# A four-branch inference step on one core: readiness kept by an account, two moves from SBUF to SBUF, squares from token tiles, and one gate projection moved ahead of the attention

## The chip, the cores and the metric

One Trainium2 chip, one of its cores, one launch. The metric is the device time of the execution in microseconds. The engines are called as in the profile: PE (TensorE, matmuls), PEld (its weight loads), DVE (VectorE), ACT (ScalarE), POOL (GpSimd) and SP (SyncE, which here issues most DMAs). TensorE's clock has two levels, 1.2 and 2.4 GHz; the granted clock of a stretch is given as a share of 2.4 GHz.

## The reference

One layer over 1056 tokens: 1024 of a prompt and 32 of a second sequence that has a cache of 1024 keys. Model width 1024, eight heads of 64, 32 state-space groups of 16 channels with a complex state of 64 each.

```python
hn = _rmsnorm(x, ln_g)
q, k, v, ga, u, gs = jnp.split(hn @ w_in, ...)        # six blocks of 512 columns
att = stick-breaking attention(q, k, v)               # causal, log-sigmoid sums instead of softmax
ssm_y, h_re, h_im = _ssm_branch(u, ...)               # diagonal complex scan, gelu, GLU with w_glu
att_o = _rmsnorm(att, g_att) * silu(ga)
ssm_o = _rmsnorm(ssm_y, g_ssm) * silu(gs)
out = jnp.concatenate([att_o, ssm_o], -1) @ w_out
return x + out, k, v, h_re, h_im                      # then a final rmsnorm
```

Outputs are y, k, v and the last states of both sequences.

## The kernel before

All matmuls run on fp32 data split into a high and a low part, so each product is three matmuls (high by high, low by high, high by low). The 3072 columns of `w_in` are cut into 24 blocks of 128; `ORDER` (L58) gives the order of the blocks: u0 to u3, gs0 to gs3 (the state-space branch's gate), g0 (the attention gate of head pair 0), q0, k0, v0, and then the rest during the attention. One block is one projection: `proj` (L432) runs 72 matmuls over three chunks of 256, 384 and 416 tokens, loads the weights two blocks ahead, splits the next block, and hands each chunk to an evacuation.

**Head.** `x_split` (L211) makes `xh` and `xl` from the eight transposed tiles `xr` on ACT and DVE. `x_sq` (L216) squares each `xr` tile on ACT and adds the eight squares, three additions on POOL and four on DVE. `x_rs` (L228) sums them over the partitions by nine matmuls against ones (L234), makes the reciprocal root on POOL (`rsqrt`) and spreads it to `rsx` by transposing matmuls (L243). The order of this early work is a list, `PREP` (L35). The first two blocks u0 and u1 run interleaved in `proj_first` and are evacuated without `rsx`, to be scaled later.

**State-space branch.** Channels come in four blocks m. For each, `s_tables` (L717) builds tables W, rot, dec and V on DVE; `s_mats` (L791) transposes W to WT, forms a small matrix Ms and sends it through DRAM into the Toeplitz operand Tm; `u_store` (L838) writes the evacuated u to DRAM (`ud`) and `u_load` (L889) reads it back as U with 8 time steps times 16 channels on the partitions; `s_states` (L898) multiplies WT by U on PE and scans on DVE; `s_out` (L942) multiplies Tm by U and V by the states, applies gelu and moves Y through DRAM (`yd`) to `yj`, from which ACT writes `y_nat`. After m = 3 `open_glu` (L1016) loads and splits `w_glu`, `glu` (L1060) runs three chunks, and `ssm_gate` (L1092) multiplies with the gate.

**Order.** Nothing is scheduled by a compiler: each engine runs its instructions in the order in which the program emits them. These pieces are generators ("links"). `tick` (L399) is called after each step of a projection (three matmuls); it resumes every link whose wait is over. A link waits for a flag of another link or for a number of ticks, and the numbers stand in a table written by hand, `WAIT` (L42). `slot` (L994) runs a projection with ticks; `until("G")` ticks until the GLU's weights are there.

**Attention.** `weave` (L1520) runs two streams. The main one is `pipeline`: for each head pair and each block of 256 queries scores on PE, two sigmoids on ACT, a scan on DVE, a product on POOL or DVE, transposes, a split on ACT and DVE, and the product with v. The fill is the list of the remaining projections, v1, q1, k1, g1, v2, q2, k2, g2, v3, q3, k3, g3 and the state-space half of the output projection. For each unit of main PE work the weave takes so much fill as `RATIO` (L47) says. A fill entry can wait for a flag: v2 waits for `att0`, the end of pair 0's last block, which comes two units into pair 1. `_layout` stores the blocks of `w_in` in the order of `ORDER`.

Of the kernel before, what the change touches and what calls it, by code (L numbers as in the profile page):

```python
# [15 lines left out]
D = 1024  # L16
# [25 lines left out]
WAIT = {'md': (0, 0, 6, 0), 'Tm': (11, 14, 6, 0), 'ud': (1, 1, 0, 4), 'ul': (8, 3, 1, 1), 'yd': (1, 0, 3, 2), 'yj': (5, 0, 1, 3), 'W': (1, 7, 1, 4), 'U': (8, 8, 3, 12), 'b': (2, 1, 1, 1), 'S': (1, 5, 1, 1), 'V': (4, 1, 4, 1), 'glu': (14, 11, 10), 'T': (1, 4, 3, 1), 'y': (17, 10, 16, 20), 'gate': (9, 9, 7, 8)}  # L42
# [15 lines left out]
ORDER = [f"{n}{m}" for n in "us" for m in range(4)] + [f"g{p}" for p in EARLY] + ["q0", "k0", "v0"]  # L58
for _p in range(1, 5):
    ORDER += ["v1"] if _p == 1 else []  # L60
    ORDER += [] if _p - 1 in EARLY else [f"g{_p - 1}"]
    ORDER += [f"v{_p}"] if 1 < _p < 4 else []
    ORDER += [f"q{_p}", f"k{_p}"] if _p < 4 else []


@with_exitstack
def hymba_step(ctx, tc, xT, xn, w_in, ln_g, kcT, vc, w_glu, b_glu, w_out, g_att, g_ssm, final_g,
               prm, h0, bmat, cvec, cbd, dsk, consts_in,
               y_out, kT_out, vT_out, st_out):
    nc = tc.nc  # L70
# [301 lines left out]
    for md in mds:  # L372
        nc.sync.dma_start(md[128:256], zz)
# [1540 lines left out]
```

## Time and profile before

| | us |
|---|---|
| median of three runs | 704.28 (703.28 to 706.74) |
| profiled execution, its time | 704.95 |
| its span, first to last instruction | 703.1 |
| PE busy in it | 634.0 |
| DVE busy | 508.2 |
| ACT busy | 352.7 |
| POOL busy | 241.6 |

The span is what the profile's rows add up to; 1.85 us of the profiled execution lie outside it. A busy PE is not the same as a fast one: at the lower clock the same matmul takes up to twice as long, so the granted clock is read beside the busy time.

### The profile page before, as it was taken

What the parts mean: (1) busy time and instruction counts of PE and PEld (TensorE: products, weight loads), DVE (VectorE), ACT (ScalarE), POOL (GpSimd) and SP (SyncE); (2) the same over time, 40 slices, a digit from 0 to 9 for tenths busy, and PEclk for the clock granted to TensorE, in tenths of its full rate; (3) what the DMA queues carried; (4) which work ended last, traced back from release to release, by engine and by line L of the source; (5) the groups of instructions that cost most, each with busy time, mean ns of one, the idle gap of its engine ahead of it and who ended that gap; (6) DMA issues with size and microseconds to landing.
All of it is one profiled execution on the core that took longest, in us unless ns stands there. A gap on an engine that the chain in (4) does not pass through costs nothing.

```text
span 703.1 us, 10847 instructions
## 1 busy us (share of the span) xinstructions
PE 634.0 (90%) x3834; PEld 570.9 (81%) x3834; DVE 508.2 (72%) x751; ACT 352.7 (50%) x805; POOL 241.6 (34%) x369
## 2 busy tenths in 40 slices
PE   7877699989999998999899998978987898989995
PEld 7877489878999997899798988967886676777884
DVE  5987999895154483687787768777778959785554
ACT  6533232431354563567665665546765746632332
POOL 0510110100123367253344326341317424233784
PEclk8998899998999998999999999999999899999998
DMA  8303514723621072101121012303253673527662
GB/s 299 85 31 77 154 31 119 243 87 97 194 68 43 25 259 109 48 31 57 62 80 55 30 62 80 106 13 99 64 155 100 191 250 110 172 93 220 216 191 97
DMA packets 62645, 79.14 MB, mean 113 GB/s; under 512 B 8864, under 2 KB 47072, under 8 KB 62592
## 3 DMA queue, kind: packets, MB, share of 16 engines
q1 hardware_dynamic: 56112, 66.90, 29.8%
q10 hardware_dynamic: 6480, 11.56, 5.2%
q8 instruction: 30, 0.49, 0.3%
q14 instruction: 23, 0.19, 0.1%
HBM read 51.97 MB, written 26.48 MB: 112 GB/s over the span
## 4 chain that ended last, share of the span: by engine, by line
PE 28%; DVE 11%; ACT 5%; issue 4%; POOL 1%; DMA 1%; DVEq 0%; ACTq 0%; POOLq 0%
PE pj L1625 8%; PE pj L439 7%; DVE cb L1207 4%; PE z L1625 4%; DVE wtl L97 3%; PE pv L1269 3%; PE tr L1306 2%; PE z L1162 2%; ACT wth L94 2%; DVE kv_out L97 1%; DVE betaL L97 1%; PE z L1358 1%; ACT cb L94 1%; DMA kc_raw<-in_vc 1%; DVE attT L97 1%
## 5 line engine op out<-in xcount | busy, mean ns | idle before, releaser
L439 PE MATMUL pj<-xh,w_hi 128*128 128x256 f32 (+2 forms) x456 | 159.7, 350 | 0.9 <-DVE kv_out L97 0.9
L439 PE MATMUL pj<-xl,w_hi 128*128 128x256 f32 (+2 forms) x456 | 148.8, 326 | 0.0
L439 PE MATMUL pj<-xh,w_lo 128*128 128x256 f32 (+2 forms) x456 | 148.3, 325 | 0.0
L1207 DVE TENSOR_TENSOR_SCAN cb<-cb 128x896 f32<-128x896 f32 (+8 forms) x66 | 96.6, 1471 | 4.7 <-ACT cb L94 4.6
L439 PEld LDWEIGHTS pj<-xh,w_hi 128*128 128x128 f32 x456 | 88.5, 194 | 5.6 <-issue 2.4
L439 PEld LDWEIGHTS pj<-xl,w_hi 128*128 128x128 f32 x456 | 88.2, 194 | 1.5
L439 PEld LDWEIGHTS pj<-xh,w_lo 128*128 128x128 f32 x456 | 87.6, 192 | 0.3
L97 DVE TENSOR_TENSOR wtl<-tr,wth 128x512 fp32r<-128x512 f32 (+2 forms) x86 | 53.5, 625 | 31.5 <-ACT wth L94 30.7
L94 ACT ACTIVATE cb<-z 128x512 f32<-128x512 f32 (+4 forms) x102 | 49.7, 487 | 47.9 <-PE z L1164 15.0
L1625 PE MATMUL pj<-xh,S 128*128 128x512 f32 (+3 forms) x212 | 69.5, 407 | 0.5 <-ACT w_raw L94 0.5
L97 POOL TENSOR_TENSOR betaL<-betaL,cb 128x896 f32<-128x896 f32 (+2 forms) x24 | 42.2, 1760 | 73.7 <-DVE cb L1207 54.4
L97 POOL TENSOR_TENSOR w_lo<-w_raw,w_hi 128x512 fp32r<-128x512 f32 x30 | 49.2, 1640 | 41.7 <-ACT w_hi L94 41.7
L97 POOL TENSOR_TENSOR betaS<-betaS,cb 128x128 f32<-128x128 f32 (+3 forms) x32 | 28.0, 880 | 74.0 <-DVE cb L1207 42.6
L94 ACT ACTIVATE wth<-tr 128x512 fp32r<-128x512 f32 (+2 forms) x86 | 47.2, 550 | 11.5 <-PE tr L1306 9.7
L1306 PE MATMUL tr<-ident,betaL 128*128 128x128 f32 x208 | 35.0, 288 | 13.1 <-DVE wtl L97 9.3
L1269 PE MATMUL pv<-wth,vS 128*128 128x256 f32 x160 | 43.9, 297 | 2.4 <-POOL wth L1246 2.4
L1625 PE MATMUL pj<-xl,S 128*128 128x512 f32 (+3 forms) x112 | 43.8, 394 | 0.2 <-DVE xl L97 0.2
L1625 PEld LDWEIGHTS pj<-xh,S 128*128 128x128 f32 (+2 forms) x212 | 37.7, 191 | 7.3 <-ACT w_raw L94 0.8
L1269 PE MATMUL pv<-wtl,vS 128*128 128x256 f32 x160 | 42.3, 286 | 0.0
L1306 PEld LDWEIGHTS tr<-ident,betaL 128*128 128x128 f32 x208 | 25.9, 147 | 17.8 <-DVE wtl L97 10.9
L97 DVE TENSOR_TENSOR kv_out<-pj,rsx 128x256 f32<-128x256 f32 (+2 forms) x55 | 28.2, 513 | 15.0 <-PE pj L439 13.9
L94 ACT ACTIVATE betaL<-z 128x512 f32<-128x512 f32 (+4 forms) x70 | 35.9, 512 | 0.0
(339 smaller groups left out, 1514.3 us busy)
## 6 DMA issues: line engine op xcount, KB each, us to landing
w_raw<-in_w_in ACTq DMA_DIRECT2D x44, 256.0 KB, 2.6
x<-in_xn SPq DMA_DIRECT2D x8, 512.0 KB, 5.1
yp_d<-x SPq DMA_DIRECT2D x8, 512.0 KB, 5.2
x<-yp_d SPq DMA_DIRECT2D x8, 512.0 KB, 4.4
y_out<-x SPq DMA_DIRECT2D x8, 512.0 KB, 2.9
xr<-in_xT SPq DMA_DIRECT2D x7, 528.0 KB, 8.5
wraw<-in_w_out SPq DMA_DIRECT2D x5, 512.0 KB, 6.6
ud<-uj SPq DMA_DIRECT2D x4, 532.0 KB, 5.6
```

The costliest lines, as they stand in the source:

```text
L94: nc.scalar.activation(out, in_, f, **kw)
L97: (eng or nc.vector).tensor_tensor(out, a, b, op)
L439: nc.tensor.matmul(ps[:, :n], a[:, k], b[:, k, t0:t0 + n], start=(k == 0 and f == 0), stop=(k == KT - 1 and f == 2))
L1162: nc.tensor.matmul(ps[:, :nn], a, b, start=(i == 0), stop=(i == len(mms) - 1 and mask is None))
L1207: nc.vector.tensor_tensor_scan(cc[:, ::-1], cc[:, ::-1], cc[:, ::-1], 1.0, OP.mult, OP.bypass)
L1269: nc.tensor.matmul(st["ps"][:, 0:256], vs[:, kb, 128 * h:128 * h + 128], w[:, c0:c0 + 256], start=(st["n"] == 0), stop=(st["n"] == 2 * nbl ...
L1306: nc.tensor.transpose(pp[:, c0:c0 + 128], b[:, 128 * kb:128 * kb + 128], ident)
L1358: nc.tensor.matmul(ps, a, b, start=(i % 2 == 0 and n == 0), stop=(i % 2 == 1 and n == 2))
L1625: nc.tensor.matmul(ps[:a.shape[1], :m], a, b_, start=(k == 0 and f == 0), stop=(k == 3 and f == len(mms) - 1))
```

## The change

1. Every link's wait is now a moment and not a number of ticks. A class `Clock` wraps the engines and keeps an account: for each emitted instruction it works out when its engine, operands and buffers would be free, by a price for each kind of instruction. `at(tiles)` waits until the account's PE time reaches the moment when the tiles are written; `dve()` until DVE's queue is within 1 us of empty. `tick` resumes a link as long as its wait is over. `WAIT` is gone. Where no projection runs, each tick adds 400 ns to the account's PE time.
2. u goes from `uj` to U, and Y to `yj`, by eight DMAs of one eighth each, from SBUF to SBUF, without DRAM.
3. The squares come from token tiles: nine tiles of x with tokens on the partitions are loaded into the freed `xr` buffers, and ACT squares each with a sum along the row, straight into the nine columns that `rsqrt` reads. The additions and the matmuls against ones are gone. `x_rs` is spawned at step 28 instead of 52, `angles` at 22 instead of 45.
4. `s_tables` is cut in two; the second half (rot, dec, V) has its own waits, and its tables have two buffers where needed. Small loads (kidx, bm, h0t, dst) are issued earlier. The GLU's weights are loaded and split by a link of their own before y3 is there.
5. The gate projection g1 leaves the attention's fill and runs after v0, ahead of the attention (`LATE`).

```diff
-RSS = 52
-RSW = 60
+RSS = 28
...
-PST = 45
+PST = 22
...
-WAIT = {'md': (0, 0, 6, 0), 'Tm': (11, 14, 6, 0), ...
+LATE = (1,)
+ORDER = [f"{n}{m}" for n in "us" for m in range(4)] + [f"g{p}" for p in EARLY] + ["q0", "k0", "v0"] + [f"g{p}" for p in LATE]
...
+class Clock:
...
+    def cost(self, e, f, n, out, ins, args):
+        if e == "PE":
+            if f == "transpose":
+                return 109.0
+            if ins[1].dtype == F32:
+                return max(1.77 * n, 100.0)
+            return 0.4414 * n + 6
+        if e == "ACT":
+            return 180 + 0.83 * n
...
+        if f == "tensor_tensor_scan":
+            return 80 + 2.09 * n
+        if f in ("tensor_scalar", "tensor_copy"):
+            return 90 + 0.55 * n
+        return (150 if f == "scalar_tensor_tensor" else 80) + 1.04 * n
...
+        if f == "dma_start":
+            b = 4 * size(out) * out.ap[0][1]
+            end = max(start + 2000 + b / 180, self.dma + b / 395)
+            self.dma = max(self.dma, start) + b / 395
+            self.t[e] = start + 340
...
+    def ready(self, *aps):
+        return max(self.last(self.w, *self.span(a)) for a in aps)
...
-    def x_sq(k):
-        act(xr[k], xr[k], AF.Square)
-        if 0 < k < 4:
-            tt(xr[0], xr[0], xr[k], OP.add, nc.gpsimd)
-        elif k > 4:
-            tt(xr[4], xr[4], xr[k], OP.add)
-        if k == 7:
-            tt(xr[0], xr[0], xr[4], OP.add)
+    def x_load(b):
+        m, c = blk(b)
+        xq[b] = xp.tile([128, D], F32, name="xq", tag=f"xr{b % KT}")
+        nc.sync.dma_start(xq[b][:m], xn[c])
+    def x_sq(b):
+        m, _ = blk(b)
+        nc.scalar.activation(xq[b][:m], xq[b][:m], AF.Square, accum_out=rst[:m, 1, b:b + 1])
...
         for b in range(9):
-            m, c = blk(b)
-            nc.tensor.matmul(ps[:m, b:b + 1], sq[:, c], ones, start=True, stop=True)
-        nc.vector.tensor_copy(rst[:, 1, 0:8], ps[:, 0:8])
+            if b == 1:
+                x_load(8)
+            yield at(xq[b], lead=XL)
+            x_sq(b)
         rsqrt(rsc, rst[:, 1], 1.0 / D, rst[:, 0], rst[:, 1])
-        yield RSW - now[0]
+        yield at(rsc)
...
         for t in list(tasks):
+            while True:
+                w = t[0]
+                if (w not in done) if isinstance(w, str) else (w() > nc.now()) if callable(w) else (w > now[0]):
+                    break
...
+    def at(*aps, lead=0.0):
+        return lambda: nc.ready(*aps) - lead
+    def dve(*aps):
+        return lambda: max([nc.t["DVE"]] + [nc.ready(a) for a in aps]) - BACK
...
         def u_store(m, uj):
-            UD[m] = dram.tile([8, 128, NCH], F32, name="ud", bufs=4)
-            nc.sync.dma_start(UD[m].rearrange("j p n -> p j n"), uj)
+            yield from after("X", m - 2)
+            yield at(uj, lead=300.0)
+            U = ss.tile([128, 8, NCH], F32, name="U", bufs=2)
+            for j in range(8):
+                nc.sync.dma_start(U[16 * j:16 * j + 16], uj[:, j])
...
         def s_states(m):
-            yield f"U{m}"
-            yield WAIT["U"][m]
+            yield f"u{m}"
             yield f"T{m}"
-            yield WAIT["T"][m]
             yield from after("Y", m - 2)
+            U, WT = z["U"], z["WT"]
+            yield at(U, WT)
...
-            yd = dram.tile([128, 8, NCH], F32, name="yd", bufs=2)
-            nc.sync.dma_start(yd, Y)
+            yield at(Y, lead=300.0)
             yj = ss.tile([128, 8, NCH], F32, name="yj", tag="uj", bufs=2)
-            nc.sync.dma_start(yj, yd.rearrange("(i c) g n -> (c g) i n", c=16))
+            for i in range(8):
+                nc.sync.dma_start(yj[:, i], Y[16 * i:16 * i + 16])
...
+        def glu_weights():
+            for f in ("V3", "T3", "B3"):
+                yield f
+            s2a.close()
+            gw = s1.enter_context(tc.tile_pool(name="gw", bufs=1, side="right"))
...
         def until(f):
             while f not in done:
+                nc.t["PE"] += 400.0
                 tick()
...
+        for i, p in enumerate(LATE):
+            slot(n + 3 + i, proj(GA[p], ga_evac(p, kvst)))
...
     def gate(p, **kw):
-        return [] if p in EARLY else [proj(GA[p], ga_evac(p, kvst), **kw)]
+        return [] if p in EARLY + LATE else [proj(GA[p], ga_evac(p, kvst), **kw)]
```

## Rows read from the trace of the kernel before

**Rows 1.** The profile page: the granted clock and the moved GB/s in 40 equal slices of 17.6 us, and the chain of waits by engine.
```profile
PEclk8998899998999998999999999999999899999998
...
GB/s 299 85 31 77 154 31 119 243 87 97 194 68 43 25 259 109 48 31 57 62 80 55 30 62 80 106 13 99 64 155 100 191 250 110 172 93 220 216 191 97
...
PE 28%; DVE 11%; ACT 5%; issue 4%; POOL 1%; DMA 1%; DVEq 0%; ACTq 0%; POOLq 0%
```

**Rows 2.** Busy time by stage. Columns: stretch, its length, then for each engine the busy us and the number of instructions, the mean granted clock, DMA share and GB/s.
```profile
20.00:40.00 20.00, 16.62 (x93) 15.83 (x91) 18.90 (x39) 10.21 (x15) 7.67 (x8) 0.91 0.20 53
...
40.00:100.00 60.00, 46.88 (x300) 41.66 (x300) 53.82 (x106) 19.14 (x62) 9.11 (x19) 0.86 0.32 86
100.00:160.00 60.00, 56.88 (x383) 49.83 (x384) 54.93 (x66) 21.11 (x56) 3.44 (x10) 0.96 0.42 132
160.00:265.60 105.60, 105.24 (x661) 102.65 (x661) 53.38 (x77) 48.55 (x88) 32.26 (x25) 0.99 0.35 116
265.60:640.00 374.40, 337.27 (x2070) 302.53 (x2068) 280.50 (x381) 220.93 (x518) 148.87 (x185) 0.96 0.30 94
```

**Rows 3.** The timeline of PE from 20 to 160 us, the instructions before which PE stood idle, and the matmuls against ones. Columns: start, us, line and operation, in brackets the idle us before it and what ended them.
```profile
27.59 0.57 PE L464 MATMUL z<-xl,w_hi 128*128 128x256 f32 x2 [2.74 <-DVE xl L214]
...
41.74 0.39 PE L439 MATMUL z<-xh,w_lo 128*128 128x256 f32 x1 [2.38 <-DVE w_lo L97]
...
44.92 2.35 PE L234 MATMUL tr<-ones,xr 128*128 128x1 f32 x18
...
51.56 0.71 PE L243 MATMUL tr<-ident,rsc 128*128 128x128 f32 x4 [1.28 <-POOL rsc L97]
...
61.07 1.09 PE L802 MATMUL tr<-ident,W 128*128 128x128 f32 x4 [3.58 <-DVE W L97]
...
81.71 1.15 PE L912 MATMUL tr<-U,WT 128*64 128x133 f32 x8 [6.52 <-DMA U<-ud]
...
101.44 0.63 PE L802 MATMUL tr<-ident,W 128*128 128x128 f32 x4 [0.92 <-DVE W L97]
...
154.82 1.89 PE L964 MATMUL z<-bst,V 64*128 64x133 f32 x8 [2.15 <-DVE bst L97]
```

**Rows 4.** The timeline of DVE from 8 to 62 us.
```profile
16.28 0.42 DVE L97 TENSOR_TENSOR w_lo<-w,w_hi 128x256 fp32r<-128x256 f32 x1
...
18.34 2.71 DVE L97 TENSOR_TENSOR w_lo<-w,w_hi 128x256 fp32r<-128x256 f32 x1
20.97 2.87 DVE L271 SCALAR_TENSOR_TENSOR P<-P 128x16 f32<-128x16 f32 x3
23.88 2.44 DVE L103 TENSOR_SCALAR P<-P 128x16 f32<-128x16 f32 x1
26.23 1.31 DVE L214 SCALAR_TENSOR_TENSOR xl<-xr,lng,xh 128x1056 fp32r<-128x1056 f32 x1
...
35.73 5.34 DVE L97 TENSOR_TENSOR xr<-xr,xr 128x1056 f32<-128x1056 f32 x4
```

**Rows 5.** The timeline of POOL from 0 to 110 us.
```profile
17.80 5.59 POOL L97 TENSOR_TENSOR xr<-xr,xr 128x1056 f32<-128x1056 f32 x2 [16.91 <-ACT xr L94]
...
47.61 0.65 POOL L103 TENSOR_SCALAR rst<-rst 128x9 f32<-128x9 f32 x1 [19.01 <-DVE rst L236]
...
51.31 0.20 POOL L97 TENSOR_TENSOR rsc<-rsc,rst 128x9 f32<-128x9 f32 x1
```

**Rows 6.** The timeline of ACT from 8 to 62 us: the first square of an x tile, and the last piece of `rsx`.
```profile
12.88 1.07 ACT L94 ACTIVATE xr<-xr 128x1056 f32<-128x1056 f32 x1
...
56.24 0.51 ACT L94 ACTIVATE rsx<-tr 128x416 f32<-128x416 f32 x1
```

**Rows 7.** The timeline of the SP queue from 0 to 110 us: when it issued the last x tiles, and u of the first two blocks to and from DRAM.
```profile
8.85 2.10 SPq L365 DMA_DIRECT2D xr<-in_xT  x3
...
63.46 1.26 SPq L842 DMA_DIRECT2D ud<-uj  x2
...
74.04 0.38 SPq L894 DMA_DIRECT2D U<-ud  x1
```

**Rows 8.** DMA issues of the whole run. Columns: what, queue, count, KB each, median us from issue to landing.
```profile
xr<-in_xT SPq DMA_DIRECT2D x7, 528.0 KB, 8.5
...
ud<-uj SPq DMA_DIRECT2D x4, 532.0 KB, 5.6
U<-ud SPq DMA_DIRECT2D x4, 532.0 KB, 5.6
...
md<-Ms SPq DMA_DIRECT2D x4, 64.0 KB, 1.5
```

**Rows 9.** The instructions on the tile `uj`: one group. Columns: count, shortest, median and longest in ns.
```profile
L97 DVE TENSOR_TENSOR uj<-pv,rsx x3: 197/834/877, 77.2 to 90.7; 128x384 f32<-128x384 f32 x2, 128x32 f32<-128x32 f32 x1
```

**Rows 10.** Busy time (columns as in rows 2) of one dense projection, gs3, and of the stretch from the end of k1 to the start of v2, in which g1 is the fill.
```profile
181.00:192.70 11.70, 11.70 (x75) 11.65 (x74) 2.87 (x5) 3.51 (x4) 2.82 (x4) 1.00 0.66 199
332.90:358.90 26.00, 22.78 (x147) 21.19 (x146) 19.78 (x27) 15.49 (x36) 11.13 (x11) 0.93 0.19 62
```

**Rows 11.** The timeline of PE: the first wait of the attention, and the first of pair 1.
```profile
271.92 0.80 PE L1162 MATMUL z<-kA,qA 128*128 128x512 f32 x1 [2.98 <-ACT betaL L94]
...
338.14 0.44 PE L1162 MATMUL z<-kA,qA 128*128 128x384 f32 x1 [2.41 <-ACT kA L94]
```

**Rows 12.** The timeline of POOL from 228 to 298 us: the last of the four gate products of the state-space branch.
```profile
265.44 2.47 POOL L97 TENSOR_TENSOR y_nat<-y_nat,sgs 128x1056 f32<-128x1056 f32 x1
```

More of the change, by code (lines that the diff above doesn't have):

```diff
@@ new lines, with __init__, manual_schedule, tile_pool @@
+class TimedPools:
+    def __init__(self, clock, tc):
+        self.clock, self.tc, self.nc = clock, tc, tc.nc
+    def manual_schedule(self):
+        return self.tc.manual_schedule()
+    def tile_pool(self, name, bufs=1, **kw):
+        return TimedPool(self.clock, self.tc.tile_pool(name=name, bufs=bufs, **kw), name, bufs)
+class TimedPool:
+    def __init__(self, clock, pool, name, bufs):
+        self.clock, self.pool, self.name, self.bufs = clock, pool, name, bufs
+    def __enter__(self):
+        self.ctx, self.pool = self.pool, self.pool.__enter__()
+        return self
+    def __exit__(self, *a):
+        return self.ctx.__exit__(*a)
+    def tile(self, shape, dtype, name, tag=None, bufs=None, **kw):
+        t = self.pool.tile(shape, dtype, name=name, **({} if tag is None else {"tag": tag}),
+                           **({} if bufs is None else {"bufs": bufs}), **kw)
+        self.clock.buffer((self.name, tag or name), bufs or self.bufs, t.tensor.name if hasattr(t, "tensor") else t.name)
+        return t
@@ L66, in hymba_step, with __init__, __getattr__, call @@
+class Timed:
+    def __init__(self, clock, eng, name):
+        self._c, self._e, self._n = clock, eng, name
+    def __getattr__(self, f):
+        g = getattr(self._e, f)
+        if f == "lower_ap" or not callable(g):
+            return g
+        def call(*args, **kw):
+            self._c.run(self._n, f, args, kw)
+            return g(*args, **kw)
+        return call
 @with_exitstack
@@ L291, in exp_ @@
         yield
[L292 removed]
+        ki = sa.tile([128, 16], I32, name="ki")
         nc.vector.tensor_copy(ki, t1)
@@ L715, in angles, with two, three @@
             done.add("pc")
+        sh = [128, 8, 8, 16]
+        def two(t, i, c=None):
+            a = t[:, i:i + 2].rearrange("p r q k -> p (r q) k")
+            return (a if c is None else a[:, :, c][:, :, ::-1])[..., None].to_broadcast(sh)
+        def three(t):
+            return t.rearrange("p r q c -> p (r q) c")[:, :, None, :].to_broadcast([128, 12, 8, 16])
         def s_tables(m):
@@ L756, in s_tables, with s_tables2 @@
-            z.update(cb=cb, W=W)
-            done.add(f"W{m}")
-            FT = ss.tile([128, 3, 4, 8], F32, name="FT")
+                pass
+            z.update(cb=cb, W=W, Pm=Pm, cv=cv)
+            yield at(cb, cv)
+            ts(cb[:, 1], cb[:, 1], -1.0, None, OP.mult, None, gp)
+            ts(cv[:, 1], cv[:, 1], -1.0, None, OP.mult, None, gp)
+            gp.tensor_copy(cv[:, 2], cv[:, 0])
+            done.add(f"W{m}")
+        def s_tables2(m):
+            z = M[m]
+            g = slice(4 * m, 4 * m + 4)
+            yield f"W{m}"
+            yield from after("S", m - 2)
+            Pm, cv = z["Pm"], z["cv"]
+            FT = sa.tile([128, 3, 4, 8], F32, name="FT")
```

306 lines of the change are left out of this document (173 added, 133 removed).

## The prediction, made before the changed kernel ran

> **What bounds the kernel now.** I read the stages first, because one share for the whole run hides them. From 160 to 265.6 us PE is busy 105.24 of 105.6 us at a granted clock of 0.99 [rows 2]: there PE alone sets the time, with DVE at half load, so whatever reaches PE sooner in that stretch is worth nothing by itself. Before 160 us it is another picture: PE is idle in 20 to 160 us by 3.4, 13.1 and 3.1 us, its clock is 0.91, 0.86 and 0.96, and DVE is busy 127.65 of 140 us. So I went to the timeline of PE for that stretch and took each wait with its releaser [rows 3]. Seven of them make 2.74 + 2.38 + 1.28 + 3.58 + 6.52 + 0.92 + 2.15 = 19.57 us, and every one ends with DVE, with POOL's root or with the landing of U. The chain of waits, the last view, has PE with 28% of the span [rows 1] and is followed back only as far as the attention; for the head it says nothing.
>
> The low clock belongs to the waits. In 20 to 100 us it is lowest where the waits are; where PE runs without one (160 to 265.6) it is 0.99. What it costs I estimate as busy time by missing share [rows 2]: 0.09 x 16.62 + 0.14 x 46.88 + 0.04 x 56.88 = 1.5 + 6.6 + 2.3 = 10.4 us.
>
> **Squares from token tiles.** POOL adds squares from 17.80 us on [rows 5], and in that time DVE's instructions stretch: a split of 256 columns that takes 0.42 us takes 2.71, four tiny ones 5.3 [rows 4]. From 18.34 to 26.23 DVE does what unhindered would be some 1.3 us of work, so POOL costs it 6.6 us; its own four additions cost 5.34 more. The first loss is behind PE's wait of 2.74 us (DVE's split of x starts at 26.23), the second behind the wait of 2.38 (the split of w stands behind the additions). Both go. So do the 2.35 us of matmuls against ones [rows 3].
>
> Added are nine squares on ACT with a sum along the row. The form is in no row I read; its bounds are the plain square, 1.07 us [rows 6], and twice that. I take the plain one, about what is removed; even doubled, 9 us more fit into the time that ACT is idle (busy 10.21 of 20 us and 19.14 of the next 60 [rows 2]). Added too are nine loads on SP, 4.33 MB, which wait for the split of the x tile in whose buffer they go; behind the waiting one stand only tables' loads and the u moves, needed later. The last x tile is issued by 10.95 us and lands 8.5 later [rows 7, 8], so the tokens flow from about 19.4 us; at the 299 GB/s of the page's first slice [rows 1] they need 14.5 us, until 34. A square, POOL's root (47.61 to 51.51, 3.9 us [rows 5]) and the spreading (51.56 to 56.75, 5.2 us [rows 3, 6]) then give `rsx` at about 44 us and not 56.75. If the loads ran at half that rate it would be 58, about as before; u2 and u3, two projections of 11.7 us [rows 10], cover PE until then.
>
> **u and Y from SBUF to SBUF.** Before, u of the first block is issued at 63.46 and PE has U at 81.71 [rows 7, 3]: 18.2 us for a store, a wait in ticks and a load. Now there are eight issues of 66 KB. Issues in a row took 0.63 to 0.70 us each, a single one 0.38 [rows 7]; the nearest size, 64 KB, landed in 1.5 us [rows 8]. Bounds: 8 x 0.38 + 1.5 = 4.5 and 8 x 0.70 + 1.5 = 7.1; I take 6.5, by 0.63. The account has 8 x 0.34 + 2.4 = 5.1, so PE may wait 1.4 us at each U. Four times that is 5.6 us. The Y move saves as much time, but at a place where PE does not wait [rows 2]; I cost it at nothing, hidden by the gate and q, k, v projections.
>
> The Trainium skill, "DMA: Bandwidth & Descriptors", sections "Anatomy of one DMA" and "Bandwidth", speaks against cutting a move in eight: it gives about 2.0 us fixed for each DMA and asks for large ones. Against it stand the x tiles here, of which three were issued within 2.10 us while each takes 8.5 to land [rows 7, 8]: transfers of one queue overlap. If those 2.0 us of the Trainium skill were paid eight times in a row, a move would take 16 us and the sum below would be 38 us higher.
>
> **Links by account.** PE's waits for W (3.58, 0.92), for U (6.52) and for the scan (2.15) are instructions put in PE's queue before their data were there. With `at`, PE gets projections meanwhile, of which there are enough: ten of 11.7 us. Those waits go, unless the account is ahead of the chip. It prices a scaling of u of 384 columns at 80 + 1.04 x 384 = 479 ns; the row has 834 [rows 9]. On some 12 such instructions it falls 4.3 us behind DVE. A wait puts PE behind by just as much, so waits cannot add up to more than that shortage. New waits then: 5.6 + 4.3, about 10 us (bounds 2 and 20: the faster issue and no shortage; twice both).
>
> **g1 ahead of the attention.** In front it is a dense projection, 11.7 us [rows 10], on PE where PE is the bound. Out of the attention it leaves the stretch from k1 to v2, 26.0 us with PE busy 22.78 and DVE 19.78; v2 can't move up, as it waits for `att0`. If DVE keeps all its 19.78 us, the stretch gives back 6.2; if g1's part of it goes, which I estimate as twice gs3's 2.87 (scaling, and the products of the gate), it shrinks to 14.0 and gives 12.0. I take 8.5, since the wait for kA (2.41 us [rows 11]), which is not g1's, stays and is no longer filled. The start of the attention gains: its first wait, 2.98 us [rows 11], falls while POOL still multiplies the state-space gate (at 265.44 [rows 12]), and the clock is 0.8 in that slice [rows 1], another 2 us or so. With an earlier branch and g1 in between, this is over: 4 us, bounds 0 and 5.
>
> **The sum**, against the profiled execution's own 704.95: minus 19.6 (waits), minus 2.35 (matmuls), minus 10.4 (clock), plus 10 (new waits), plus 11.7 - 8.5 (g1), minus 4 (start) = 681.9. That execution is 0.67 above the median of the runs, so I predict **681.3 us**, 3.3% faster. The new waits alone span 673 to 691; with g1's and the start's bounds the case's own range is 671 to 693.
>
> **Rivals.**
> - *DVE sets the pace anyway.* DVE is busy 91% of 20 to 160 us and all links end on it. The change takes 6.6 + 5.34, about 12 us, off it; if that is all PE gets and the other 20 us of the gain come back as idle PE between links, the time is 704.28 - 12 + 11.7 - 8.5 - 4 = 691.5, with the g1 bounds 688 to 699. For it: DVE's load. Against: PE has projections to run in the meantime, and DVE is half idle from 160 us on, so that the branch may end later without PE running dry.
> - *No change.* The same, with g1 at its dearest (+5.5) and no better start: 12 - 5.5, 697.8, and a few us more of new waits: 699 to 707.
> - *Slower: the account runs ahead of the chip.* To pass 707.8 us the new waits must grow from 10 to 36.5 us. At 0.36 us a piece that takes about 100 mispriced instructions out of the 172 that DVE runs in 40 to 160 us [rows 2]. For it: the one price that I could hold against a row is off by 74%. Against: most are of other shapes. About 712.
> - *Slower: the eight parts of a move run one after the other.* 8 x 1.5 = 12 us [rows 8] instead of 5.1, so 7 us at each of four U's, 28 instead of 5.6: 703.7; from 1.65 us a part on it is past 707.8. By the Trainium skill's 2.0 us for each DMA (the page named above) it would be 719.
>
> **How the numbers follow.** The forecast 0.60, DVE's pace 0.20, no change 0.08, account 0.08, series (1.65 us a part or more) 0.04. A measurement of this kernel tells about 0.5% (3.5 us) from no change. Faster 0.80, same 0.08, slower 0.12. The range that leaves out no more than 2 in 10 goes from 668 to 701: it takes in the first two cases, with a little below for a better g1.
>
> **What would show it.** Right: no idle of PE over 2 us between 25 and 160 us; clock there 0.95 or more; `rsx` written by 46 us; the first `s_states` matmul by 56 us; the first score matmul of the attention by 255 us although g1 stands in front of it; k1 to v2 in 16 to 20 us. Wrong: PE waits for U of more than 3 us (series), idle PE spread over 40 to 160 us with DVE above 95% (DVE's pace), or k1 to v2 above 20 us (g1's hole is dearer than I think).

## The result, and the profile after

The changed kernel takes 711.97 us (median of four runs, 708.22 to 713.85), the kernel before 703.78 on the same chip (700.90 to 706.74): a ratio of 1.0113, with 1.0076 to 1.0149 as its 95% interval. It is slower by 1.1%; 681.3 us was forecast, with 668 to 701 as the range. The profiled execution took 708.22 us (span 706.4), the lowest of the four, so its trace holds 3.3 us of the loss against the span of before (703.1), and what the other runs lose beyond that no row shows. Almost all instructions are recorded at line L212, the account's wrapper, so tiles tell the groups apart.

Busy time of the changed kernel in the stages of [rows 2], columns as there:
```profile
20.00:40.00 20.00, 13.88 (x87) 13.50 (x85) 14.32 (x63) 13.22 (x26) 0.00 (x0) 0.95 0.72 262
40.00:100.00 60.00, 55.26 (x373) 50.74 (x374) 49.12 (x75) 21.18 (x67) 8.84 (x23) 0.93 0.29 83
100.00:160.00 60.00, 56.64 (x389) 50.04 (x388) 50.06 (x60) 20.00 (x55) 3.15 (x10) 0.97 0.42 105
160.00:265.60 105.60, 99.56 (x603) 96.12 (x604) 51.60 (x76) 50.48 (x91) 32.29 (x25) 0.97 0.33 99
```
DVE is relieved in the first three (127.65 us busy before, 113.50 now) and POOL's squares are gone. Yet PE is idle by 6.1, 4.7, 3.4 and 6.0 us, together 20.3 us, about the sum of [rows 2] (3.4, 13.1, 3.1, 0.4: 20.0 us). The idle time has moved, not gone. PE's waits in 20 to 280 us (columns: instruction, releaser, us in total, times, longest):
```profile
PE z L212 <- ACT w_hi L212: 7.8, 1, 7.8
PE tr L212 <- DMA U<-uj: 3.3, 2, 2.1
PE tr L212 <- DVE W L212: 3.0, 1, 3.0
PE z L212 <- ACT Y L212: 3.0, 1, 3.0
PE z L212 <- ACT betaL L212: 2.4, 1, 2.4
PE z L212 <- ACT yh L212: 1.8, 1, 1.8
PE z L212 <- DVE yl L212: 1.3, 2, 0.9
```
They make 22.6 us, and in the same stretch the kernel before waits 23.0. Of the seven waits of [rows 3] four are gone. Three stand in another size: u2 waits 7.83 us for its split of w (2.38, and it gets going at 41.7 us in both kernels), the first W is waited for 3.03 us (3.58), and U in two places, 2.06 and 1.28 (6.52). The other entries lie behind that stretch. The largest is read on ACT's timeline:
```profile
26.29 1.06 ACT L212 ACTIVATE xq<-xq 128x1024 f32<-128x1024 f32 x1 [5.80 <-DVE P L212]
27.26 0.18 ACT L212 ACTIVATION_READ_ACCUMULATOR xq<-xq 128x1 f32 x1
...
40.00 1.04 ACT L212 ACTIVATE xq<-xq 32x1024 f32<-32x1024 f32 x1
...
41.04 1.13 ACT L212 ACTIVATE w_hi<-w_raw 128x512 fp32r<-128x512 f32 x2
```
u0 and u1 end at 33.9 us (before 39.1), and then u2 waits until 41.70 for its split of w. It stands in ACT's queue behind nine squares (1.06 us and 0.18 for the sum each), the first of them at 26.29, and behind some 4 us of tables and evacuations between them.

Where the time went, stage by stage: v0 ends at 257.2 us (before 263.4), 6.2 earlier, all of it busy time (216.94 us of PE from 20 us on, before 223.43: the matmuls against ones and some clock). Then g1 takes 12.1 us, its price in front, as forecast. The attention starts at 271.6, 2.4 us behind g1 (2.8 us behind v0 before), v1 to k1 takes 67.2 us (66.4), and the stretch from k1 to v2, which [rows 10] has at 26.0 us, takes 23.9 (counted like these 23.9, from the end of k1's last matmul, it was 26.3):
```profile
257.10:269.20 12.10, 12.10 (x79) 12.04 (x78) 5.32 (x8) 3.59 (x8) 5.95 (x4) 1.00 0.47 175
...
338.80:362.70 23.90, 15.30 (x77) 12.13 (x76) 18.83 (x23) 13.90 (x33) 7.42 (x9) 0.79 0.10 32
```
PE has 7.48 us less to do there than in the 26.0 of [rows 10], and the stretch is 2.4 us shorter. DVE keeps 18.83 of its 19.78 us, PE's wait for kA grows from 2.41 [rows 11] to 4.02:
```profile
344.42 0.44 PE L212 MATMUL z<-kA,qA 128*128 128x384 f32 x1 [4.02 <-ACT kA L212]
```

### The profile page after: what moved, and what is told of

Its sections match the earlier page's. It is cut to its first block, busy times and chain, and to the rows that moved or that the text cites. A ratio compares the mean times of both kernels' runs of the same rounds, so it can differ in the third digit from the quotient of the medians.

```text
span 706.4 us, 10910 instructions
## 1 busy us (share of the span) xinstructions
PE 631.3 (89%) x3816; PEld 565.1 (80%) x3816; DVE 499.3 (71%) x745; ACT 357.3 (51%) x817; POOL 228.7 (32%) x366
## 4 chain that ended last, share of the span: by engine, by line
PE 47%; DVE 19%; ACT 10%; POOL 7%; issue 7%; DMA 7%; SPq 2%; ACTq 0%; DVEq 0%; POOLq 0%
PE pj L212 22%; PE z L212 12%; PE pv L212 7%; PE tr L212 6%; DVE cb L212 6%; DVE wtl L212 3%; SPq L212 2%; ACT wth L212 2%; DMA xr<-in_xT 2%; DVE kv_out L212 2%; POOL rst L212 2%; DVE attT L212 2%; POOL betaL L212 1%; DMA U<-uj 1%; DMA xq<-in_xn 1%
## 5 line engine op out<-in xcount | busy, mean ns | idle before, releaser
L212 PE MATMUL pj<-xh,w_hi 128*128 128x256 f32 (+2 forms) x472 | 161.6, 345 | 1.0 <-DVE kv_out L212 1.0
L212 PE MATMUL pj<-xl,w_hi 128*128 128x256 f32 (+2 forms) x472 | 152.0, 325 | 0.0
L212 PE MATMUL pj<-xh,w_lo 128*128 128x256 f32 (+2 forms) x472 | 151.8, 324 | 0.0
L212 DVE TENSOR_TENSOR_SCAN cb<-cb 128x896 f32<-128x896 f32 (+8 forms) x66 | 100.4, 1528 | 3.6 <-ACT cb L212 3.4
L212 PEld LDWEIGHTS pj<-xh,w_hi 128*128 128x128 f32 x472 | 91.0, 193 | 4.6 <-issue 1.6
L212 PEld LDWEIGHTS pj<-xl,w_hi 128*128 128x128 f32 x472 | 90.7, 192 | 1.5
L212 PEld LDWEIGHTS pj<-xh,w_lo 128*128 128x128 f32 x472 | 89.8, 190 | 0.3
L212 DVE TENSOR_TENSOR wtl<-tr,wth 128x512 fp32r<-128x512 f32 (+2 forms) x86 | 53.6, 626 | 31.7 <-ACT wth L212 30.9
L212 ACT ACTIVATE cb<-z 128x512 f32<-128x512 f32 (+4 forms) x102 | 49.7, 487 | 51.8 <-PE z L212 23.3
L212 PE MATMUL pj<-xh,S 128*128 128x512 f32 (+3 forms) x212 | 69.1, 405 | 0.5 <-ACT w_raw L212 0.5
L212 POOL TENSOR_TENSOR betaL<-betaL,cb 128x896 f32<-128x896 f32 (+2 forms) x24 | 42.2, 1759 | 83.7 <-DVE cb L212 37.6
L212 POOL TENSOR_TENSOR w_lo<-w_raw,w_hi 128x512 fp32r<-128x512 f32 x30 | 45.5, 1516 | 62.8 <-ACT w_hi L212 62.8
L212 PE MATMUL tr<-ident,betaL 128*128 128x128 f32 x226 | 38.4, 286 | 15.8 <-DVE wtl L212 10.6
L212 ACT ACTIVATE wth<-tr 128x512 fp32r<-128x512 f32 (+2 forms) x86 | 47.3, 551 | 9.2 <-PE tr L212 6.3
L212 POOL TENSOR_TENSOR betaS<-betaS,cb 128x128 f32<-128x128 f32 (+3 forms) x32 | 27.9, 879 | 70.6 <-DVE cb L212 51.1
L212 PE MATMUL pv<-wth,vS 128*128 128x256 f32 x160 | 45.2, 303 | 2.6 <-POOL wth L212 2.6
L212 PEld LDWEIGHTS tr<-ident,betaL 128*128 128x128 f32 x226 | 27.5, 145 | 22.6 <-DVE wtl L212 13.3
L212 PE MATMUL pj<-xl,S 128*128 128x512 f32 (+3 forms) x112 | 43.7, 393 | 0.8 <-DVE xl L212 0.8
L212 PEld LDWEIGHTS pj<-xh,S 128*128 128x128 f32 (+2 forms) x212 | 37.9, 191 | 7.5 <-ACT w_raw L212 0.8
L212 PE MATMUL pv<-wtl,vS 128*128 128x256 f32 x160 | 42.9, 290 | 0.4 <-DVE wtl L212 0.4
L212 ACT ACTIVATE betaL<-z 128x512 f32<-128x512 f32 (+4 forms) x70 | 35.9, 513 | 0.0
L212 PEld LDWEIGHTS pv<-wth,vS 128*128 128x128 f32 x160 | 31.8, 199 | 3.7 <-POOL wth L212 2.9
```

Source lines behind the costliest of these rows:

```text
L212: return g(*args, **kw)
```

## The experiments

Every ratio is to the kernel before, run beside it on the same chip, with its 95% interval.

### g1: back in the attention, and alone in front

```diff
-LATE = (1,)
+LATE = ()                    # e1: changed kernel, g1 back between k1 and v2
```


> The changed kernel with g1 put back into the attention, between k1 and v2; links by account, moves in SBUF and squares from token tiles stay. Theory (g1 ahead of the attention is a loss by itself: it cost 12.1 us in front, and k1's end to v2's start only fell from 26.0 to 23.9 us): the time falls by 8 to 11 us against the changed kernel, to about 702 us, a ratio of 0.995 to 1.000 to the kernel before; k1's end to v2's start goes back to about 26 us. Rival (the prediction's: the attention pays for the gate what the front saves): the time stays within 3.5 us of the changed kernel's 712, and k1 to v2 grows by 8 us or more.

```diff
+LATE = (1,)                  # e2: kernel before, g1 behind v0
-ORDER = ... + ["q0", "k0", "v0"]
+ORDER = ... + ["q0", "k0", "v0"] + [f"g{p}" for p in LATE]
...
```


> The kernel before with that one part of the change alone: g1 runs behind v0, ahead of the attention; S5 links, DRAM round trips and squares are as before. Theory (loss by itself): 7 to 11 us slower than before, about 712 us, ratio 1.010 to 1.015, g1 about 12 us in front and k1 to v2 still over 22 us. Rival (neutral): ratio within 0.5% of 1, k1 to v2 about 16 to 18 us.

e1: 1.0015 (0.9987 to 1.0043) of before, so 1.0% below the changed kernel. e2: 1.0082 (1.0051 to 1.0112). Both say the same: g1 in front is a loss of 6 to 7 us, between the two expectations and clear of "neutral". In e2 the stretch from k1 to v2 takes 22.8 us (26.3) with DVE busy 17.75, so what it gives back is 3.5 us and not 8.5. The start of the attention did gain there: v1 begins 0.3 us behind g1 (2.8 behind v0), v1 to k1 takes 62.8 us, and from v0's end to k1's end it is 77.1 us, only 8 more than before (69.2) although g1 lies in it. In the changed kernel it is 81.6, and the gain is missing: the last gate product ends at 271.8 us, before at 267.9. That is not because the whole branch is late, for the third product ends at 262.0 us, 2.3 earlier than before. POOL of the changed kernel:
```profile
259.55 2.46 POOL L212 TENSOR_TENSOR y_nat<-y_nat,sgs 128x1056 f32<-128x1056 f32 x1 [1.26 <-PE tr L212]
...
268.14 1.30 POOL L212 TENSOR_TENSOR w_lo<-w_raw,w_hi 128x512 fp32r<-128x512 f32 x1 [4.88 <-ACT w_hi L212]
269.40 2.42 POOL L212 TENSOR_TENSOR y_nat<-y_nat,sgs 128x1056 f32<-128x1056 f32 x1
```
The fourth product stands behind a split of the next weights, on POOL, and its sigmoid behind the other half of that split on ACT (267.43), for whose load ACT sat 2.03 us.

### The moves of u and Y

```diff
+            ud = dram.tile([8, 128, NCH], F32, name="ud", bufs=4)
+            nc.sync.dma_start(ud.rearrange("j p n -> p j n"), uj)
+            yield at(ud[0:8], lead=500.0)
-            for j in range(8):
-                nc.sync.dma_start(U[16 * j:16 * j + 16], uj[:, j])
+            nc.sync.dma_start(U, ud.rearrange("j (c g) n -> (j c) g n", g=8))
...                                              # e4: the same for Y; e6: u alone
```


> The changed kernel with u and y moved through DRAM again, as in the kernel before (one DMA out, one back, each link resumed by the account when the first should be there). Theory (the eight issues for each move hold SP for 6 us and the buffer of uj is held by them): VectorE's wait of 6.13 us at 59.5 us goes, the last W of chunk m = 0 is done before 62 us instead of 64.8, and the time is 0 to 5 us lower than the changed kernel's. Rival (the prediction's: SBUF to SBUF is the shorter way): each move lands 3 to 5 us later than in the changed kernel, and the time is 2 to 8 us higher.

> The changed kernel with u alone through DRAM; y goes from SBUF to SBUF, and g1 stays in front. Theory (it is the move of u, whose eight issues for each chunk hold SP and the two buffers of uj while the projections still write u): most of the gain of the run with both through DRAM comes, a ratio of 1.000 to 1.004 to the kernel before. Rival (it is the move of y, which makes the branch's tail long): 1.008 to 1.012, like the changed kernel.

e4: 1.0001 (0.9978 to 1.0023), 1.1% below the changed kernel and more than the theory's 0 to 5 us, so the two moves through SBUF together are a loss. The issues and landings of the changed kernel, then of e4 (columns as in [rows 8]):
```profile
U<-uj SPq DMA_DIRECT2D x32, 66.5 KB, 2.7
yj<-Y SPq DMA_DIRECT2D x32, 66.5 KB, 2.5
```
```profile
ud<-uj SPq DMA_DIRECT2D x4, 532.0 KB, 5.1
U<-ud SPq DMA_DIRECT2D x4, 532.0 KB, 3.5
```
And the changed kernel's SP queue and DVE in 48 to 66 us:
```profile
51.84 12.43 SPq L212 DMA_DIRECT2D U<-uj  x16
```
```profile
49.13 3.60 DVE L212 TENSOR_TENSOR uj<-uj,rsx 128x384 f32<-128x384 f32 x6 [0.97 <-ACT rsx L212]
...
59.46 0.64 DVE L212 TENSOR_TENSOR uj<-z,rsx 128x256 f32<-128x256 f32 x1 [6.13 <-DMA U<-uj]
...
63.57 1.23 DVE L212 TENSOR_TENSOR W<-W,tW 128x1024 f32<-128x1024 f32 x1
```
The sixteen parts of the first two blocks take 12.43 us of the queue, with a stop of 2.2 us behind the eleventh. `uj` has two buffers, and u2's scaling, third in turn, waits until the last part of u0 has landed: DVE sits 6.13 us, and the three instructions of the first W stand behind it (done at 64.8 us, before the change 60.9). In e4 a store frees `uj` in one piece, that wait is not there, W is done at 58.8, the first states come at 67.2 us instead of 73.7, and the last `y_nat` ends at 191.8 instead of 196.8. A Y move is no shorter in SBUF: from the last gelu to `y_nat` 8.1 us (186.4 to 194.5), in e4 7.5.

The Trainium skill, "DMA: Bandwidth & Descriptors", sections "Anatomy of one DMA" and "Bandwidth", asked for large DMAs because of a fixed time of each. Its figure of about 2.0 us is given for DMAs that GpSimd issues; here SP issues them. These traces don't show it paid eight times in a row: the move of u0 took 7.6 us, not 16, since parts overlap. What they show is the queue and the buffer held meanwhile.

e6 has neither expectation: 1.0202 (1.0179 to 1.0225), slower than with both moves in SBUF. Up to 118 us it runs as e4; then the first Y is thought to land sooner than it does. ACT and DVE of e6:
```profile
126.99 2.07 ACT L212 ACTIVATE y_nat<-yj 128x1024 f32<-128x1024 f32 x1 [2.66 <-DMA yj<-Y]
```
```profile
137.05 0.29 DVE L212 TENSOR_TENSOR Ms<-Ms,dd 32x128 f32<-32x128 f32 x1 [5.67 <-ACT Ms L212]
```
`y_nat` stands on ACT ahead of evictions of the next states, Ms comes later, and DVE, with the small instruction on Ms at its head, sits 5.67 us (e4: 1.00) with S of the second block behind it. S of the last block ends at 186.5 us, in e4 at 171.4. The early gain of e4 is in e6 too (first states at 67.5 us) and did not make it faster. So the wait at `uj` alone does not explain e4, and no run shows that u's move by itself is a loss.

### Squares later, and squares as before

```diff
-XL = -1500.0
+XL = -7000.0          # e3: changed kernel; e7: with g1 back and both moves through DRAM
```


> The changed kernel with the account's start of the squares of x put 5.5 us later, so that ScalarE's queue has the split of w for the third u projection ahead of most of them. Theory (ScalarE's order makes TensorE's wait of 7.83 us at 41.7 us): that wait falls below 4 us, u2 ends 3 to 6 us earlier, and the time falls by 3 to 6 us if the stage that follows is not held by something else. Rival (the S5 chain on VectorE and its DMAs set the end of the stage): the wait falls but the first score matmul comes no more than 1.5 us earlier, since later waits grow by the same.

> The run with g1 back and both moves through DRAM, and the squares of x 5.5 us later in the account as in the third experiment. Theory (the squares' place on ScalarE only shifts a wait: TensorE's wait for the split of w at 41 us shrinks by 5 us or more, but rsx and with it the first W come later by as much): within 3 us of the run with g1 back and both moves through DRAM. Rival (the third experiment lost its 12 us to the moves of u alone, and the later squares are a gain once those are gone): 3 to 6 us faster than that run.

> Links by account alone: g1 back, both moves through DRAM, and the squares of x taken from the transposed tiles on ScalarE with adds on GpSimd and VectorE and the nine sums over TensorE, as in the kernel before. What is left of the change is the account, with the small loads moved ahead. Theory (the squares from token tiles give the 5 us by which the first two u projections end earlier, of which half is lost again at ScalarE): 2 to 4 us slower than the run with g1 back and both moves through DRAM, a ratio of 0.993 to 0.997 to the kernel before. Rival (the squares' part is worth nothing or is a loss, by the wait of 7.83 us at ScalarE): as fast as that run or up to 4 us faster.

e3: 1.0244 (1.0214 to 1.0275). PE's largest hole is cut to a third, u2 ends 5 us earlier, and the kernel is 1.3% slower than the changed one. PE of e3, and its busy time in 180 to 200 us:
```profile
37.33 0.39 PE L212 MATMUL z<-xh,w_hi 128*128 128x256 f32 x1 [2.64 <-ACT w_hi L212]
...
69.45 0.36 PE L212 MATMUL pj<-xh,w_hi 128*128 128x256 f32 x1 [3.67 <-DVE uj L212]
```
```profile
180.00:200.00 20.00, 16.60 (x83) 13.84 (x83) 8.06 (x10) 6.55 (x14) 0.00 (x0) 0.51 0.35 72
```
`rsx` is whole at 54.5 us instead of 50.7, W of the first block comes at 74.2 (64.8), the last `y_nat` at 207.1 (196.8). PE has run out of projections by 171.6 us and starts q0 at 197.1, with the outputs of the branch alone in between at a clock of 0.51. So the theory fell: the wait at u2 was not on the path. The rival held in kind, but what took its place was more than as much: the first score matmul comes 9.4 us later.

e7 is 1.0108 (1.0080 to 1.0136) where e5, the same without the later squares, has 0.9952: a loss with the DRAM moves too. e8, the account with the squares as in the kernel before, is 1.0196 (1.0161 to 1.0231): `rsx` at 61.6 us, the last `y_nat` at 211.4. Squares from token tiles are worth 2.4% to this account, and the account without them is a loss of 2%, by far more than either expectation. Neither of the two runs came out as its theory or its rival said.

### Both undone

> The changed kernel with two parts undone: g1 back between k1 and v2, and u and y through DRAM as before. The links by account and the squares from token tiles stay. Theory (each of the two parts is a loss of its own, and they add): g1 alone gave a ratio of 1.008 on the kernel before and cost 1.0 per cent on the changed one, the moves cost 1.1 per cent on the changed one, so the ratio to the kernel before falls to about 0.990 (0.986 to 0.994, about 699 us). Rival (both runs won the same thing: any relief ahead of the attention, and the attention's own start sets the rest): ratio 0.997 to 1.003.

e5, e1's and e4's edits together: 0.9952 (0.9929 to 0.9976). Faster than the kernel before, but by half of what the sum of the parts says. (The traced execution, 705.45 us, is one of the slowest of twelve with a median of 701.35, so its rows don't hold the gain.) v0 ends at 253.1 us (263.4 before), and then:
```profile
PE z L212 <- ACT betaL L212: 9.5, 1, 9.5
```
Of the 10.3 us that PE gained ahead of the attention it waits 9.5 (before 2.98 [rows 11]) for the branch.

### The order of the links

```diff
-            yield dve(Ms)
+            yield at(Ms, lead=-1500.0)          # e11, on the changed kernel
```


> The changed kernel with one link of the account emitted later: the two small VectorE instructions on Ms (dd and Ms) when the account has Ms 1.5 us behind it, instead of 1 us ahead of VectorE's own turn. Theory (links emitted ahead of their input hold VectorE's whole queue: it sat 4.5 us in this one at 132 to 136.6 us, with the E of the third chunk behind it): VectorE's wait for Ms falls from 5.1 to below 2 us, S of the third chunk comes 3 us or more earlier than 153.1 us, and the time falls by 2 to 4 us. Rival (the order of all later links shifts with it and takes it back): the wait goes and the time stays within 2 us or grows.

```diff
+            at_step(1, 0, spawn, s_tables2(m))
             at_step(1, 1, spawn, s_states(m))
-            at_step(1, 1, spawn, s_tables2(m))  # e12, on the changed kernel
```


> The changed kernel with the tasks of the rotations and of V asked before the tasks of the states at each turn, so that V of the last two chunks can be emitted ahead of S, not behind it, where it adds 3.6 us between S and the first output product. Theory (V behind S lengthens the tail): V of the last chunk ends before S, the last y_nat comes 2 to 4 us earlier than 196.8 us, the time falls by 1 to 4 us. Rival (VectorE's sum is the same, so that S only comes later by what V takes ahead of it): within 1.5 us of the changed kernel.

Each was aimed at a hole that its row shows: DVE 4.52 us idle ahead of Ms, and V behind S in the last block, on the changed kernel's DVE:
```profile
136.59 0.29 DVE L212 TENSOR_TENSOR Ms<-Ms,dd 32x128 f32<-32x128 f32 x1 [4.52 <-ACT Ms L212]
...
168.14 1.33 DVE L212 TENSOR_TENSOR bst<-bst,st_t 128x536 f32<-128x536 f32 x2
169.39 1.22 DVE L212 TENSOR_TENSOR tW<-Pm,cv 128x1024 f32<-128x1024 f32 x1
```
e11: 1.0221 (1.0182 to 1.0261), e12: 1.0401 (1.0354 to 1.0449). In e11 the waits for Ms leave the list, but PE's product takes the place at DVE's head, and W of the last block comes at 144.9 us (127.0). In e12 V of the last block does end ahead of S, at 174.9 us, but S only at 202.2 (169.5). DVE's waits in 20 to 200 us, of e11 and of e12:
```profile
DVE kv_out L212 <- PE pv L212: 6.2, 4, 3.0
```
```profile
DVE kv_out L212 <- PE pv L212: 8.9, 2, 5.1
DVE Ms L212 <- ACT Ms L212: 6.7, 2, 6.2
```
The rival of e11 holds, and e12 is worse than its rival. One link moved shifts later ones, and another instruction without its input comes to stand at the head of a queue. With shifts of 1 to 3% from one link, a difference of 1% between two orders, such as that of e4, need not be the price of the part that was changed.

### The tail ahead of the attention

```diff
-                tt(yv, yv, sg, OP.mult, gp)
+                tt(yv, yv, sg, OP.mult)         # e9 on e5; e14 on the kernel before
```


> The run with g1 back and both moves through DRAM (0.995 of the kernel before), and in its last step ahead of the attention the four products of y with the gate on VectorE instead of GpSimd, where they take 2.45 us each and follow one another every 3.7 us. Theory (the tail of the branch, not TensorE, sets the start of the attention; TensorE waits 9.5 us for betaL there): the last product ends 3 to 5 us earlier than 264.0 us, the wait shrinks by as much, and the time falls by 2 to 4 us, a ratio of 0.990 to 0.993. Rival (TensorE's own work sets it): the ratio stays at 0.995.

> The kernel before with one edit: the four products of y with the gate on VectorE instead of GpSimd. Theory (the branch's tail sets the start of the attention in the kernel before as well, so that TensorE's holes ahead of it were not the path alone): the last product ends 2 to 4 us earlier than 267.9 us, TensorE's wait of 2.98 us for betaL shrinks, and the time falls by 1.5 to 4 us, a ratio of 0.994 to 0.998. Rival (the prediction's reading: TensorE sets it, the branch has room): a ratio of 0.999 to 1.003.

e9: 0.9881 (0.9841 to 0.9922). DVE's part of the gate beside POOL's products in e5, and in e9:
```profile
254.45 3.29 DVE L212 SCALAR_TENSOR_TENSOR y_nat<-y_nat,gssm,gs 128x1056 f32<-128x1056 f32 x1
```
```profile
254.55 1.30 DVE L212 SCALAR_TENSOR_TENSOR y_nat<-y_nat,gssm,gs 128x1056 f32<-128x1056 f32 x1
255.96 1.26 DVE L212 TENSOR_TENSOR y_nat<-y_nat,sgs 128x1056 f32<-128x1056 f32 x1
```
A product takes 1.26 us there instead of 2.45, DVE's own instruction 1.30 instead of up to 3.29, and the last product ends at 259.8 us (264.0). PE's wait for betaL is 1.8 us:
```profile
PE z L212 <- ACT betaL L212: 1.8, 1, 1.8
```
One instruction's engine, with no work of PE touched, gives 0.7%, with intervals that just part; the attention starts 4.2 us earlier (263.9, in e5 268.0): in e5 the branch's tail sets the end. The Trainium skill, "SBUF — State Buffer", section "SBUF: two separate sides", states that a VectorE instruction with two inputs in SBUF and a GpSimd one that reads SBUF lock each other out for a whole instruction. These rows agree, with 1.30 us alone and 3.29 beside a product.

The same edit on the kernel before, e14: 0.9974 (0.9946 to 1.0002), a ratio inside the theory's numbers, but the interval touches 1. Its last product ends only 1.0 us earlier (266.9), and the attention starts at 271.9 as before. The wait of 2.98 us for betaL is gone, and in 255 to 285 us PE waits instead:
```profile
PE tr L540 <- DVE kv_out L97: 1.8, 2, 1.6
PE z L1162 <- ACT betaS L94: 1.4, 1, 1.4
```
Whether before has any room there stays open.

### An earlier start

```diff
-    nc.sync.dma_start(gatt, g_att)             # with gssm, bglu, h0t, dst, md
...
             w_load(o[1])                       # end of the PREP loop
+    nc.sync.dma_start(gatt, g_att)             # e10 on e5; e13 on e9
```


> The run with g1 back and both moves through DRAM, with seven small loads (gatt, gssm, bglu, h0, d, two zero blocks), which stand between 16.1 and 24.2 us on SP, put behind the loads of the token tiles. Theory (rsx, which every u and so every state waits for, starts the chain that sets the end of the branch): the first square starts 4 to 7 us earlier than 27.9 us, rsx is whole at 47 to 50 us instead of 53.7, TensorE's wait of 9.7 us for the split of w shrinks, and the time falls by 3 to 6 us. Rival (the chain regains it at its next hold): rsx comes earlier but the last y_nat within 2 us of 193.5 us, and the time does not move.

> The run with g1 back and both moves through DRAM (0.995 of the kernel before), with both edits that were each a gain: the gate products on VectorE (0.988) and the token tiles loaded ahead of seven small loads (0.987). Theory (two places: one shortens the tail ahead of the attention, the other shortens TensorE's wait at the third u projection and starts the chain earlier): they add, a ratio of 0.978 to 0.984. Rival (one place: what the earlier squares gain reaches the attention only by the tail, or was not there): 0.985 to 0.990.

e10: 0.9871 (0.9827 to 0.9914), e13: 0.9888 (0.9847 to 0.9929). The first square starts at 22.3 us, 5.6 earlier, but the last ends only at 39.9, since ACT's other work comes between, and `rsx` is whole at 51.5. PE's wait at u2 shrinks (to 5.4 us in e13, 9.1 in e9) and e13 gains nothing on e9. Its waits for w and for betaL:
```profile
PE z L212 <- ACT w_hi L212: 5.4, 1, 5.4
...
PE z L212 <- ACT betaL L212: 3.9, 1, 3.9
```
The last `y_nat` is at 191.3 us in e13 and 190.8 in e9, and what PE saved at u2 it waits in part at betaL: the rival of "one place" holds for e13. The gain of e10 by itself, 0.8% on e5 with intervals that just part, its own trace explains in part: the last `y_nat`, the last product and the attention come 2.3 to 2.4 us earlier than in e5, of some 5.7 us.

## Why the prediction was wrong

Four terms of its sum failed. PE's waits did not shrink by 9.6 us but stayed at 20, the clock gave back 4 us and not 10.4, the stretch that g1 left gave back 2.4 us and not 8.5, and the start of the attention gained nothing instead of 4. Behind the first stands that new waits were bounded by the moves of u and the account's error on `uj` alone, where 7.83 us came from ACT's order. And of the ten projections that were to fill the waits three, q0, k0 and v0, stand behind `until("G")`, and so behind the last Y of the state-space branch; in six of the runs below PE ran out of the others.

What the time goes by can be read off all sixteen traces at once (us from the span's start; "attention" is the third score matmul, the first that a wait for betaL precedes in the kernel before [rows 11]):

| kernel | rsx whole | last y_nat | first glu matmul | attention | span | ratio |
|---|---|---|---|---|---|---|
| before | 56.8 | 188.3 | 201.9 | 271.9 | 703.1 | 1 |
| e14 | 55.5 | 189.4 | 202.8 | 271.9 | 702.8 | 0.9974 |
| e9 | 51.6 | 190.8 | 191.9 | 263.9 | 695.7 | 0.9881 |
| e10 | 51.5 | 191.1 | 192.3 | 265.8 | 700.3 | 0.9871 |
| e13 | 51.2 | 191.3 | 192.5 | 264.3 | 696.3 | 0.9888 |
| e5 | 53.7 | 193.5 | 194.6 | 268.0 | 703.7 | 0.9952 |
| e1 | 53.2 | 200.3 | 201.8 | 274.0 | 705.3 | 1.0015 |
| e7 | 56.5 | 201.3 | 202.5 | 277.1 | 708.3 | 1.0108 |
| e8 | 61.6 | 211.4 | 212.6 | 286.1 | 717.8 | 1.0196 |
| e2, g1 in front | 56.5 | 187.3 | 200.9 | 279.6 | 707.0 | 1.0082 |
| e4, g1 in front | 52.3 | 191.8 | 192.9 | 274.2 | 706.1 | 1.0001 |
| after, g1 in front | 50.7 | 196.8 | 198.7 | 276.7 | 706.4 | 1.0113 |
| e6, g1 in front | 52.6 | 205.6 | 206.8 | 285.9 | 718.6 | 1.0202 |
| e3, g1 in front | 54.5 | 207.1 | 208.3 | 287.3 | 719.4 | 1.0244 |
| e11, g1 in front | 52.5 | 207.3 | 208.5 | 288.5 | 722.1 | 1.0221 |
| e12, g1 in front | 52.7 | 222.1 | 223.3 | 302.4 | 734.3 | 1.0401 |

The spans are of one execution each, the ratios of medians (the traced e5 is 4.1 us above its median, the traced e10 3.8). From "attention" to the end of the span it is 427 to 436 us in every row, with g1 in front (427.4 to 433.6) or not (430.9 to 435.7). From the first glu matmul to "attention" it is 69 to 75 us, with g1 in front 78 to 81. And in every kernel with the account glu follows the last `y_nat` by 1.1 to 2.0 us. So with the account the time follows the end of the state-space branch (S5) nearly one to one (e4 to e12: 30.3 us later, 28.2 us slower), whatever PE's waits are. The program makes it so, by `until("G")`: in e3, e6, e7, e8, e11 and e12 g0 is done 9 to 26 us before q0 starts, and PE has no projection in between. In the kernel before it is otherwise: `y_nat` is ready at 188.3, glu comes 13.6 us later, behind its weights (split by 197.6) and a PE that is never idle from 160 to 200 us.

Against the kernel before, the table also splits the changed kernel's loss. Its glu starts 3.2 us earlier, although its `y_nat` is later; from there to the attention it takes 8.0 us more, with g1 in it; the rest is 1.5 us shorter. Together that is the 3.3 us of the two traces, and e1 and e2 show the g1 part as a loss of its own.

By the prediction's own steps:

- **Squares from token tiles.** u0 and u1 do end 5.2 us earlier and the matmuls against ones are gone (2.35 us, as forecast). The step failed where ACT's idle time was taken as cover: the nine squares fit into it, but ACT runs in order, and the split of w for u2 stood behind them, 7.83 us. `rsx` came at 50.7 and not 44: the first token load is issued at 22.99 us, behind the small loads, and not at once.
- **u from SBUF to SBUF.** The move of u0 took 7.6 us (51.84 to 59.46, when DVE has its buffer back), forecast 6.5. The step that failed is the one left out: who waits for `uj` and for SP meanwhile. It was asked for PE's wait at U alone (5.6 us; 3.3 measured).
- **Links by account.** New waits ahead of the attention: 10 us forecast, bounds 2 and 20; PE's idle from 20 to 265.6 us is 20.3 us, where before it was 20.0. The argument that waits cannot add up to more than the account's error on `uj` left out every other queue: the largest wait (7.83 us) comes from ACT's order, and the first W is waited for as before. The clock gave back some 4 us by the busy time (6.5 less the 2.35), not 10.4. The sum took the whole missing share back, while the prediction's own sign asked for a clock of 0.95, and 0.95 is what came.
- **g1.** In front 12.1 us (11.7 forecast). Out of the attention 2.4 us, in e2 3.5, not 8.5 and below the bound of 6.2: that bound took DVE's busy time as all that the stretch needs. In the 23.9 us no engine is busy for more than 18.83, and the wait for kA grew to 4.02. The start's 4 us came in e2 and not in the changed kernel.
- **The sum.** Waits 9.9 us, clock some 6, g1's hole 6.1, its price in front 0.4 and the start some 4 us above their terms: 681.9 and 27 make 709, near the profiled execution's 708.22. The case's own range is narrow as well: its bounds added up give 669 to 698 and not 671 to 693.

Of the rivals, "DVE sets the pace" was the nearest in kind: what PE gains comes back as waits for the links. It was not DVE's load (91% busy before, 81% now), and it was priced 20 us too low; that the order in which DVE, ACT and SP get the links takes its place is what the holds in the rows above show. "The account runs ahead of the chip" names a part of it (y_nat in e6, Ms in the changed kernel). That its "about 712" is the measured time is luck: it wanted new waits of more than 36 us, where 20 came. Of the signs named, only the clock came out as forecast:
```profile
25.00:160.00 135.00, 120.78 (x815) 109.29 (x814) 108.84 (x183) 53.91 (x144) 11.99 (x33) 0.95 0.40 115
```
PE's idle of at most 2 us (7.83), `rsx` (50.7 us instead of 46), the first state matmul (73.7 instead of 56), the first score matmul (271.0 instead of 255) and k1 to v2 (23.9, above the 20 named for a dearer hole) came out against it.

Which single link puts the last `y_nat` of the changed kernel 8.5 us behind that of before is not settled. In e4, with both moves undone, it is 5 us earlier, but in e6 without the hold at `uj` it is 8.8 us later. V behind S is 3.6 us by its row, but e12, meant to take that away, could not show it. A third hold is in the trace: the last evictions of Y stand on ACT behind a split of the GLU's weights, and PE waits 2.96 us for them.
```profile
176.61 0.63 ACT L212 ACTIVATE wgh<-wgr 128x512 fp32r<-128x512 f32 x1 [2.10 <-DMA wgr<-in_w_glu]
...
180.28 0.68 ACT L212 ACTIVATE Y<-z 128x266 f32<-128x266 f32 x2
```
No run undoes the early GLU weights, the small loads or the cut of `s_tables` by themselves, so what these are worth is not shown.

## What to carry over

Idle time of the busiest engine is worth taking away only as far as the branch beside it ends earlier too: follow the side branch to its last product, and ask what it gains, before pricing the holes. Idle time of an engine that runs in order is no cover by its sum; ask what stands behind each new instruction and which buffer a transfer holds while its parts wait in the queue. The fastest kernels here (0.987 to 0.989) kept the account, the squares and the early GLU weights, and undid the moves and g1; in e9 and e13 the products on DVE came on top, in e10 and e13 the earlier token loads.

## What was not expected of the hardware

A square with a sum along the row is two records on ACT, 1.06 us and 0.18. Eight issues of 66.5 KB from SBUF to SBUF take 5.1 us of SP's queue, 0.64 each; each lands in 2.5 to 2.7 us, so that the round trip of 532 KB through DRAM (5.1 and 3.5 us, two issues) costs about the same time and a fraction of the queue.
